# Joining the low-rank query and key weights behind the seventh unit of the first token block instead of the second

## The chip, the cores and the metric

The kernel runs on one core of a Trainium2 chip. The metric is the device time of one execution in microseconds (us), as the median of several runs. The engines are TensorE (PE), whose weight loads are listed apart (PEld), VectorE (DVE), ScalarE (ACT), GpSimd (POOL) and SyncE (SP), which issues nearly all transfers here.

## What is computed

Two layers over 256 context tokens and 2048 latent tokens of width 1024. Each layer normalises and modulates its input (`adaLN`: a shift and a scale from a small matrix product with `w_mod`), projects it by one wide matrix `w_in`, feeds three groups of heads (two gated linear recurrences and one latent attention), and projects the gated results back, with a gate on the sum. The part that matters here is the latent attention's query and key:

```python
def mla_qkv(zcq, zckv, zkr, q_norm_g, kv_norm_g, w_uq, w_ukv, rope):
    q = (rms_norm(zcq, q_norm_g) @ w_uq).reshape(B, L, MLA_HEADS, MLA_QK)
    kv = (rms_norm(zckv, kv_norm_g) @ w_ukv).reshape(B, L, MLA_HEADS, MLA_NOPE + MLA_DV)
    q_nope, q_rope = q[..., :MLA_NOPE], q[..., MLA_NOPE:]
    k_nope, v = kv[..., :MLA_NOPE], kv[..., MLA_NOPE:]
...
    s = jnp.einsum('bqhd,bkhd->bhqk', q, k).astype(F32) * MLA_SCALE
```

The kernel never forms `k_nope`. It multiplies the two low-rank weights of a head once per layer, (256 x 128) times (128 x 128), and scores the 256-wide query latents against the 128-wide key latents through that product. This product is what the change moves.

## The kernel before

Each layer has three stages: `project` (L270), `mix` (the recurrences and the attention) and `output`. Matmul operands are kept as a high and a low half (`hh`/`hl` of the tokens, `wh`/`wl` of the weights), and a product is three matmuls: high x high, high x low, low x high. `split` (L75) makes the halves: a cast on ScalarE (L79), a subtract on VectorE (L85).

`project` takes the tokens in pairs of 128-token tiles, nine pairs in three blocks of three. The columns of `w_in` are cut into twelve groups of up to 256. A unit is one group for the three pairs of a block; the first block's first unit takes groups 0 and 1 together, so its unit `i` is group `i + 1`. A group and a pair make 48 matmuls into one psum tile `pj` of four (L421, or L432 for groups 2 to 5, whose result is transposed). ScalarE or VectorE empties it (L452, L457, L458, L465, L478) and SP stores it. The weights of the next group are loaded as two `wraw` tiles (L355) and split one unit ahead. Behind groups 4, 6 and 8 of a block the next block's pairs are prepared (`normed_pair`): load `xt` (L366), normalise on VectorE (L369 to L375), transpose on TensorE (L383) into one of two psum tiles with the tag `tr`, from which ScalarE writes the modulated `hf` (L390); then `split_pair` makes `hh` (L81) and `hl`. Group 0 also starts the decay gates of one recurrence (`gla_decay`, L587 to L591): for each direction VectorE, ScalarE twice, VectorE (L590), ScalarE (L591).

In layer 0 two more things go on beside the first block. `mod_rest` (L164) computes the rest of the modulation on VectorE: 64 pieces `wmt` of 128 x 512 (L184, three buffers) are loaded one after the other, and each is reduced by L187 (twice for the first 48, once for the rest). After the first sixteen pieces VectorE adds a bias (L192) and SP writes the layer's gate by two transfers (L194), each of 1024 single elements of 4 bytes to scattered addresses:

```python
                for i in range(2):
                    nc.sync.dma_start(out=S0["gate"][i].rearrange("(k p) -> p k", p=P), in_=mc[:, 0:8, i])
```

And `latent_weights` (L240) loads `uq` (L244, in one of the three `xt` buffers), `uk` (L246) and `ur` (L248, both in `stg` buffers of the pairs' results), multiplies (`pw`, L254; the trace shows sixteen records for the eight matmuls) into two psum tiles, also of the tag `tr`, and splits the product into `mh`/`ml` and `ur` into `urh`/`url`. Its results are used first in `mix` (L854, L866).

A scheduler sets the order on each engine from its own estimate of time, with the program's order as priority; SP's queue is worked in order, and at most eight of its transfers are under way.

Of the kernel before, what the change touches and what calls it, by code (L numbers as in the profile page):

```python
# [54 lines left out]
class Trunk:  # L55
# [214 lines left out]
    def project(self, l, S, after):  # L270

        nc, io = self.nc, self.io
        with ExitStack() as ctx:
            R = Route(lambda: self.pool(ctx), "hh hl", "stg gcat gq gkv",
                      "zaT ltn lkd zn zh ltt lqn jk ss rsk rsq ropt ropa ropb gxs gab",
                      "srow wmt jkm mp mc bmc bmd gcol pad", "wraw", "xt st mv ve rs hf", "wh wl")
            ps = Route(lambda: self.pool(ctx, psum=True), "tz", "pj", "tr", "px")
            npair = self.ntiles // 2
            blocks = [list(range(p0, min(p0 + 3, npair))) for p0 in range(0, npair, 3)]

            units = [(b, gs) for b in range(len(blocks))
                     for gs in ([(0, 1)] if b == 0 else [(0,), (1,)]) + [(g,) for g in range(2, self.NGROUP)]]
            h, hf, w, side = {}, {}, {}, iter(())
            if l == 0:
                nc.gpsimd.memset(R.tile([P, 32], F32, name="pad")[:, 0:1], 0.0)
                bm = self.mod_first(S, R, ps, lambda: hf.update({0: self.normed_pair(l, S, R, ps, 0, plain=True)}))
                side = self.mod_rest(S, after, R, bm)
                for g in range(2):
                    w[0, g] = self.group_weights(l, R, g, first=True)
                self.modulate(S, hf[0], 0)  # L290
            else:
                pad = R.tile([P, 64 * 64 + 40], F32, name="pad")
                nc.gpsimd.memset(pad[:, 0:1], 0.0)
                with self.tc.high_priority(offset=self.EARLY):
                    w[0, 0] = self.group_weights(l, R, 0)
                    hf[0] = self.normed_pair(l, S, R, ps, 0)
                    w[0, 1] = self.group_weights(l, R, 1)
                    h[0] = self.split_pair(R, hf[0], hi_eng="act")
                    if len(blocks[0]) > 1:
                        hf[1] = self.normed_pair(l, S, R, ps, 1)  # L300
                        h[1] = self.split_pair(R, hf[1], hi_eng="act")
            self.gate_weights(l, S, R)
            if l > 0:
                self.lower_bounds(S)
            for nm, n in (("gcat", 512), ("gq", 256), ("gkv", 128)):
                S[nm] = R.tile([P, n], F32, name=nm)
                nc.sync.dma_start(out=S[nm], in_=io[nm][l:l + 1, :].to_broadcast([P, n]))
            for pr in blocks[0]:
                if pr not in hf:
                    hf[pr] = self.normed_pair(l, S, R, ps, pr)  # L310
                if pr not in h:
                    h[pr] = self.split_pair(R, hf[pr])
            for i, (b, gs) in enumerate(units):
                nxt = blocks[b + 1] if b + 1 < len(blocks) else []
                j, r = divmod(gs[0] - (self.NGROUP - 8), 2)
                norm = r == 0 and 0 <= j < len(nxt)
                if norm:
                    hf[nxt[j]] = self.normed_pair(l, S, R, ps, nxt[j])
                    if j == 0:
                        h[nxt[0]] = self.split_pair(R, hf[nxt[0]])  # L320
                if i + 1 < len(units):
                    bn, gn = units[i + 1]
                    w[bn, gn[0]] = self.group_weights(l, R, gn[0])
                use = [self.group(l, S, R, ps, g, w.pop((b, g)), h, blocks[b]) for g in gs]
                for j, pr in enumerate(blocks[b]):
                    for u in use:
                        next(u, None)
                    if gs[-1] == self.NGROUP - 1 and j + 1 < len(nxt):
                        h[nxt[j + 1]] = self.split_pair(R, hf[nxt[j + 1]])
                for u in use:  # L330
                    for _ in u:
                        pass
                if i == 1:
                    self.latent_weights(l, S, R, ps)
                if b > 0 and not norm:
                    next(side, None)
                    next(side, None)
            for _ in side:
                pass
# [886 lines left out]
```

## Time and profile before

| | us |
|---|---|
| median of 3 runs (lowest, highest) | 3754.92 (3752.4, 3761.37) |
| the profiled execution's own time | 3755.9 |
| its span | 3754.2 |
| TensorE busy | 3612.3 |
| VectorE busy | 2139.7 |
| ScalarE busy | 1435.5 |

The mean granted clock of TensorE is 0.986 of full speed. Times in the trace count from the start of the span; in a timeline a row's bracket tells how long the engine had stood idle before it, and what ended that. Layer 0's projection goes to about 440 us, layer 1's starts near 1970.

### The profile page before, as it was taken

The page shows a single profiled execution, that of the slowest core. Times are in us where ns is not written, and L with a number is a line of the kernel's source. Part 1 is how long each engine was busy: PE and PEld are TensorE (multiplying, and loading weights), DVE is VectorE, ACT ScalarE, POOL GpSimd, SP SyncE. Part 2 cuts the span into 40 slices and gives each one's busy share as a digit, 9 for nine tenths or more (in the row PEclk, how much of TensorE's full clock was granted, in tenths as well). Part 3 has the DMA queues.
Part 4 walks back from the last instruction along what each step waited for, and adds up shares of the span by engine and source line. Part 5 has one row for each costly group of instructions (what it writes and reads, how often), then busy time and mean ns, then how long its engine had stood idle before and what let it go on. Part 6 is the DMA issues. An engine that isn't in the chain of part 4 may idle for free. (4 is left out here: it accounts for less than half of the span.)

```text
span 3754.2 us, 84546 instructions
## 1 busy us (share of the span) xinstructions
PE 3612.3 (96%) x36056; PEld 3264.7 (87%) x36056; DVE 2139.7 (57%) x5026; ACT 1435.5 (38%) x2296; POOL 811.6 (22%) x617
## 2 busy tenths in 40 slices
PE   8999999999999999998999999999999999999999
PEld 5899999888888888887879999998888888888787
DVE  6764242566666666656765442525665566656566
ACT  3525242344444444443115342523443444444400
POOL 1000000001335354341110000000022344644211
PEclk9999999999999999998999999999999999999999
DMA  7774344322122111116435443433221121221342
GB/s 253 234 202 145 126 132 143 111 81 91 49 69 84 56 61 62 55 43 206 153 110 170 146 152 108 154 120 113 83 90 43 60 68 57 78 78 44 102 143 101
DMA packets 263689, 410.79 MB, mean 109 GB/s; under 512 B 39633, under 2 KB 179985, under 8 KB 262289
## 3 DMA queue, kind: packets, MB, share of 16 engines
q1 hardware_dynamic: 261872, 403.04, 33.8%
q8 instruction: 283, 4.64, 0.5%
q10 hardware_dynamic: 1440, 2.36, 0.2%
q14 instruction: 94, 0.76, 0.1%
HBM read 288.66 MB, written 116.67 MB: 108 GB/s over the span
## 5 line engine op out<-in xcount | busy, mean ns | idle before, releaser
L421 PE MATMUL pj<-wh,hl 128*128 128x256 f32 (+1 forms) x2224 | 622.2, 280 | 7.9 <-DVE hl L85 7.9
L421 PE MATMUL pj<-wh,hh 128*128 128x256 f32 (+1 forms) x2224 | 623.9, 281 | 1.7 <-DVE ve L373 1.2
L421 PE MATMUL pj<-wl,hh 128*128 128x256 f32 (+1 forms) x2224 | 622.7, 280 | 0.1
L911 DVE TENSOR_SCALAR_CACHE_REDUCE sx<-pss 128x512 f32<-128x512 f32 (+1 forms) x648 | 402.9, 632 | 206.1 <-PE pss L909 181.7
L85 DVE TENSOR_TENSOR pl<-ptp,ph 128x512 fp32r<-128x512 f32 x580 | 389.5, 687 | 187.5 <-ACT ph L79 184.2
L79 ACT CAST ph<-ptp 128x512 fp32r<-128x512 f32 x580 | 327.9, 586 | 363.7 <-PE ptp L947 358.3
L421 PEld LDWEIGHTS pj<-wh,hl 128*128 128x128 f32 x2224 | 420.1, 189 | 8.7 <-DVE hl L85 8.6
L421 PEld LDWEIGHTS pj<-wh,hh 128*128 128x128 f32 x2224 | 421.1, 189 | 1.8 <-DVE ve L373 1.6
L421 PEld LDWEIGHTS pj<-wl,hh 128*128 128x128 f32 x2224 | 421.0, 189 | 0.6 <-issue 0.6
L947 PE MATMUL ptp<-ident,sx 128*128 128x128 f32 x2320 | 372.9, 279 | 25.4 <-DVE pl L85 15.8
L934 PE MATMUL oc<-ph,cnh 128*128 128x256 f32 x1160 | 339.6, 315 | 22.7 <-ACT ph L79 22.0
L921 ACT ACTIVATE sx<-sx,nm 128x2304 f32<-128x2304 f32 (+1 forms) x136 | 288.4, 2121 | 184.2 <-DVE nm L917 183.7
L432 PE MATMUL pj<-hh,wh 128*128 128x256 f32 x1136 | 317.3, 279 | 0.0
L947 PEld LDWEIGHTS ptp<-ident,sx 128*128 128x128 f32 x2320 | 273.2, 142 | 50.4 <-DVE pl L85 20.2
L432 PE MATMUL pj<-hh,wl 128*128 128x256 f32 x1136 | 316.2, 278 | 0.0
L432 PE MATMUL pj<-hl,wh 128*128 128x256 f32 x1136 | 315.8, 278 | 0.0
L934 PE MATMUL oc<-ph,cnl 128*128 128x256 f32 x1160 | 301.9, 283 | 0.0
L85 DVE TENSOR_TENSOR wl<-wraw,wh 128x1024 fp32r<-128x1024 f32 (+1 forms) x144 | 169.4, 1211 | 230.6 <-ACT wh L79 230.5
L905 PE MATMUL pss<-cth,qh 128*128 128x512 f32 (+1 forms) x648 | 264.9, 409 | 13.7 <-DVE sx L911 13.7
L934 PEld LDWEIGHTS oc<-ph,cnh 128*128 128x128 f32 x1160 | 222.1, 191 | 51.7 <-ACT ph L79 37.9
L939 PE MATMUL oc<-pl,cnh 128*128 128x256 f32 x1160 | 242.9, 291 | 0.0
L906 PE MATMUL pss<-ctl,qh 128*128 128x512 f32 (+1 forms) x648 | 242.9, 375 | 0.0
(253 smaller groups left out, 7888.0 us busy)
## 6 DMA issues: line engine op xcount, KB each, us to landing
wraw<-in_w_in_dram SPq DMA_DIRECT2D x132, 512.0 KB, 4.5
dnat<-stg SPq DMA_DIRECT2D x104, 256.0 KB, 2.1
vg<-dnat SPq DMA_DIRECT2D x17, 1024.0 KB, 6.1
yt<-dy SPq DMA_DIRECT2D x34, 512.0 KB, 3.6
wmt<-in_w_modT_dram SPq DMA_DIRECT2D x64, 256.0 KB, 4.0
fa<-dF SPq DMA_DIRECT2D x18, 768.0 KB, 4.5
ka<-dK SPq DMA_DIRECT2D x18, 768.0 KB, 4.2
dK<-stg SPq DMA_DIRECT2D x36, 256.0 KB, 4.6
```

The costliest lines, as they stand in the source:

```text
L79: nc.scalar.copy(hi, src)
L85: nc.vector.tensor_tensor(lo, src, hi, op=ALU.subtract)
L421: nc.tensor.matmul(pj[:, j, :n], h[pr][a][:, k, tk], w[b][:, k, :n], start=(k == 0 and a + b == 0), stop=(k == KD - 1 and a == 1))
L432: nc.tensor.matmul(pj[:, j, :], w[b][:, k, cs], h[pr][a][:, k, :], start=(k == 0 and a + b == 0), stop=(k == KD - 1 and b == 1))
L905: nc.tensor.matmul(pss[:, :n], G["qh"][hp][:, i, tk], K["cth"][:, ks], start=True, stop=False)
L906: nc.tensor.matmul(pss[:, :n], G["qh"][hp][:, i, tk], K["ctl"][:, ks], start=False, stop=False)
L911: nc.vector.tensor_scalar(sx[:, ks], pss[:, :n], SCALE, None, op0=ALU.mult, op1=ALU.max, accum_out=mx[:, nb:nb + 1])
L921: nc.scalar.activation(sx[:, :nk], sx[:, :nk], AF.Exp, bias=nm, accum_out=sm)
L934: nc.tensor.matmul(oc, K[k][:, keys(kc, c)], ph[:, c, :], start=(kc + c == 0 and k == "cnh"), stop=False)
L939: nc.tensor.matmul(oc, K["cnh"][:, keys(kc, c)], pl[:, c, :], start=False, stop=(kc + c == nch - 1))
L947: nc.tensor.transpose(pt[:, c, i, :], pexp[i][:, (kc + c) * P:(kc + c + 1) * P], self.ident)
```

## The change

One number: `latent_weights` is called behind unit 6 (group 7) of the first block in place of unit 1 (group 2), in both layers.

```diff
@@ -330,7 +330,7 @@
                 for u in use:
                     for _ in u:
                         pass
-                if i == 1:
+                if i == 6:
                     self.latent_weights(l, S, R, ps)
                 if b > 0 and not norm:
                     next(side, None)
```

What the scheduler makes of it, in layer 0. On TensorE, `pw` stood before among the matmuls of group 3's first pair, 473 `pj` matmuls into the layer:

```order
L432 MATMUL pj<-hh,wh 128x256
L432 MATMUL pj<-hl,wh 128x256
L254 MATMUL pw<-uk,uq 128x128 x8
L432 MATMUL pj<-hh,wl 128x256
L432 MATMUL pj<-hh,wh 128x256
```

It now stands among those of group 8's first pair, 1193 `pj` matmuls in:

```order
L421 MATMUL pj<-wh,hh 128x256
L421 MATMUL pj<-wl,hh 128x256
L254 MATMUL pw<-uk,uq 128x128 x8
L421 MATMUL pj<-wh,hl 128x256
L421 MATMUL pj<-wh,hh 128x256
```

Between the two, the token transposes of L383 stand where they stood (the second set behind 626 `pj` matmuls, before 623); those of the block's third pair, before ahead of the new place, now stand behind `pw`. In layer 1 `pw` moves alike, to 41 matmuls into group 8.

On SP's queue, around the gate's transfers in layer 0, before:

```order
L184 DMA wmt<-in_w_modT_dram 128x512 x2
L194 DMA gate_86<-mc 128x8x1 x2
L246 DMA uk<-in_ukT_dram 128x4x128
L248 DMA ur<-in_uqr_dram 128x2x256
L184 DMA wmt<-in_w_modT_dram 128x512 x2
L453 DMA dQ_89<-stg 128x512
L355 DMA wraw<-in_w_in_dram 128x4x256
```

and now:

```order
L184 DMA wmt<-in_w_modT_dram 128x512 x3
L194 DMA gate_86<-mc 128x8x1 x2
L184 DMA wmt<-in_w_modT_dram 128x512
L453 DMA dQ_89<-stg 128x512
L355 DMA wraw<-in_w_in_dram 128x4x256 x2
L184 DMA wmt<-in_w_modT_dram 128x512
L467 DMA dK_88<-stg 128x512
L467 DMA dF_87<-stg 128x512
L592 DMA dF_87<-gab 128x3x256
L184 DMA wmt<-in_w_modT_dram 128x512 x3
```

`uk` and `ur` are gone from here; `wraw` and `wmt` pieces move up. The two now stand behind the 58th `wmt` piece, among the stores of group 7's results (`dnat`):

```order
L184 DMA wmt<-in_w_modT_dram 128x512 x4
L485 DMA dnat_90<-stg 128x2x256
L184 DMA wmt<-in_w_modT_dram 128x512 x5
L246 DMA uk<-in_ukT_dram 128x4x128
L248 DMA ur<-in_uqr_dram 128x2x256
L485 DMA dnat_90<-stg 128x2x256
L184 DMA wmt<-in_w_modT_dram 128x512 x2
```

Before, the same stretch reads alike without the two. `uq` moves from behind the fourth `wmt` piece to behind the decay gates' stores, and the token tile that follows it is loaded that much earlier, so that two more tiles are normalised on VectorE ahead of L192.

On ScalarE, from the second direction's decay gate to the first `hf`, now:

```order
L588 ACTIVATE gab<-gab 128x768
L589 ACT_TABLE_LOAD
L589 ACTIVATE gab<-gab 128x768
L591 ACT_TABLE_LOAD
L591 ACTIVATE gab<-gab 128x768
L79 CAST wh<-wraw 128x1024 x2
L457 ACT_TABLE_LOAD
L457 ACTIVATE stg<-pj 128x512
L458 ACTIVATE stg<-pj 128x512
L390 ACTIVATE hf<-pt,shT_85,scT_84 128x256 x4
```

The sequence was the same before, with an L457 and L458 between L589 and L591, and six `hf` at its end.

## Rows read from the trace of the kernel before

**Rows 1.** The page, part 1: busy us, share of the span, instructions.
```profile
PE 3612.3 (96%) x36056; PEld 3264.7 (87%) x36056; DVE 2139.7 (57%) x5026; ACT 1435.5 (38%) x2296; POOL 811.6 (22%) x617
```

**Rows 2.** Waits of TensorE, 0 to 440 us: total us, times, longest us.
```profile
PE pw L254 <- DMA uk<-in_ukT_dram: 9.3, 1, 9.3
PE pt L383 <- DVE xt L375: 2.4, 1, 2.4
PE pj L421 <- DVE hl L85: 1.7, 2, 1.5
```

**Rows 3.** Timeline of TensorE, 112 to 132 us: start us, length us, engine, line.
```profile
126.00 3.75 PE L254 MATMUL pw<-uk,uq 128*128 128x128 f32 x16 [9.29 <-DMA uk<-in_ukT_dram]
129.41 0.56 PE L432 MATMUL pj<-hh,wl 128*128 128x256 f32 x1
```

**Rows 4.** Windows: stretch and its length; PE, PEld, DVE, ACT, POOL; PEclk, DMA, GB/s.
```profile
128.00:130.00 2.00, 2.00 (x12) 2.00 (x11) 1.99 (x6) 0.80 (x2) 0.00 (x0) 0.50 1.08 384
130.00:132.00 2.00, 2.00 (x18) 2.00 (x18) 1.30 (x3) 1.97 (x3) 0.00 (x0) 0.94 1.08 380
200.00:300.00 100.00, 99.46 (x854) 99.27 (x853) 55.19 (x133) 24.27 (x43) 3.56 (x5) 1.00 0.68 178
```

**Rows 5.** Timeline of TensorE in layer 1, 2014 to 2022 us.
```profile
2018.10 1.95 PE L254 MATMUL pw<-uk,uq 128*128 128x128 f32 x16
2019.80 0.37 PE L432 MATMUL pj<-hl,wh 128*128 128x256 f32 x1
```

**Rows 6.** Timeline of SP's queue, 103 to 131 us: the issues.
```profile
111.18 1.52 SPq L194 DMA_DIRECT2D gate<-mc  x2
112.75 0.90 SPq L246 DMA_DIRECT2D uk<-in_ukT_dram  x1
```

**Rows 7.** Transfers, 105 to 130 us: GB/s in 40 slices; KB each, us to landing.
```profile
GB/s 331 313 344 292 293 359 334 300 210 226 180 34 15 12 1 0 0 0 0 25 70 28 20 23 19 22 29 38 40 66 74 157 192 377 410 392 393 383 383 387
...
uk<-in_ukT_dram SPq DMA_DIRECT2D x1, 256.0 KB, 13.1
...
gate<-mc SPq DMA_DIRECT2D x2, 4.0 KB, 12.6
```

**Rows 8.** Tile `uk` in layer 1, 1700 to 2100 us.
```profile
DMA to landing us min/median/max: 3.3/3.3/3.3
```

**Rows 9.** Timeline of VectorE, 106 to 150 us.
```profile
121.36 0.69 DVE L187 SCALAR_TENSOR_TENSOR jkm<-wmt,srow 128x512 f32<-128x512 f32 x1 [3.99 <-DMA wmt<-in_w_modT_dram]
...
135.68 1.28 DVE L369 BATCH_NORM_STATS2 st<-xt 128x6 f32<-128x512 f32 x2
...
138.02 0.96 DVE L590 SCALAR_TENSOR_TENSOR gab<-gxs,gab 128x768 f32<-128x768 f32 x1 [1.06 <-ACT gab L589]
```

**Rows 10.** Timeline of TensorE: token transposes near 148 and near 217 us.
```profile
147.98 0.60 PE L383 MATMUL pt<-ident,xt 128*128 128x128 f32 x4
...
217.38 0.60 PE L383 MATMUL pt<-ident,xt 128*128 128x128 f32 x4
```

**Rows 11.** Timeline of ScalarE, 110 to 152 us.
```profile
141.70 0.85 ACT L591 ACTIVATE gab<-gab 128x768 f32<-128x768 f32 x1
...
146.72 2.92 ACT L390 ACTIVATE hf<-pt,shT,scT 128x256 f32<-128x256 f32 x6
```

**Rows 12.** Timeline of VectorE: the first `hh` of the next block, and L187 of piece 55.
```profile
148.69 0.69 DVE L81 CAST hh<-hf 128x1024 fp32r<-128x1024 f32 x1 [0.35 <-ACT hf L390]
...
220.83 0.68 DVE L187 SCALAR_TENSOR_TENSOR jkm<-wmt,srow 128x512 f32<-128x512 f32 x1
```

**Rows 13.** Timeline of SP's queue, 206 to 224 us.
```profile
215.09 5.51 SPq L184 DMA_DIRECT2D wmt<-in_w_modT_dram  x5
...
221.55 0.33 SPq L184 DMA_DIRECT2D wmt<-in_w_modT_dram  x1
```

**Rows 14.** The page, part 6: the `wmt` pieces, KB each, median us to landing.
```profile
wmt<-in_w_modT_dram SPq DMA_DIRECT2D x64, 256.0 KB, 4.0
```

**Rows 15.** Waits of VectorE, 185 to 222 us: total us, times, longest us.
```profile
DVE jkm L187 <- DMA wmt<-in_w_modT_dram: 5.8, 6, 2.0
```

## The prediction

> **What bounds the kernel now.** I read the page's busy times first. TensorE is busy 96% of the span [rows 1], so time is won only where TensorE stands still, or runs slowly, and lost only where it is made to. I then read what TensorE waited for from 0 to 440 us, the first layer's projection [rows 2]. The joined weights (`pw`, L254) waited 9.3 us for the transfer of `uk`; nothing else that the change could reach is over 2.4 us. The timeline [rows 3] shows the spot: nothing for 9.29 us, from 116.71 on, then sixteen `pw` matmuls from 126.00, and group 3's matmuls again from 129.41. The windows [rows 4] show the tail of it: the granted clock is 0.50 (1.2 GHz) from 128 to 130, 0.94 in the next two us, and TensorE is full later (99.46 of the 100 us from 200 on). In layer 1 the same sixteen matmuls follow their neighbours without a wait and take 1.95 us [rows 5].
>
> Why was `uk` late? SP's timeline [rows 6] has the two `gate` transfers just ahead of it: 2 x 1024 elements of 4 bytes, scattered. In the DMA view [rows 7] the traffic falls to 0 to 34 GB/s behind them, then climbs to some 390; 4 KB take 12.6 us to land, and `uk`, issued at 112.75, takes 13.1. In layer 1 it takes 3.3 [rows 8]. So `uk` is not slow, it is behind the gate scatter. The same scatter holds a `wmt` piece that VectorE needs at once: its L187 waited 3.99 us, to 121.36 [rows 9].
>
> **What the change removes.** At the old place: 9.29 us of waiting. The sixteen matmuls took 129.41 - 126.00 = 3.41 us at half clock, against 2019.80 - 2018.10 = 1.70 at full clock: 1.7 more. The next four `pj` matmuls lost 0.45. Together 11.4 us [rows 3, 5]. The matmuls themselves are only moved (1.70 us in either place), as are their two casts, two subtracts, and `urh`/`url` on ScalarE and VectorE, which run beside TensorE. That is also the most this change could give: 0.30% of the 3755.9 us of the profiled execution.
>
> **What moves with it.** (a) `uq` goes on SP's queue from far ahead of the gate scatter to far behind it. It shares three buffers with the token tiles, so a token tile is loaded and normalised earlier. VectorE then does some 2 us of normalisation (1.28 for a tile's statistics [rows 9], the rest for its scaling) ahead of the gate's addition (L192): the scatter starts some 2 us later, at about 113.3. Other splits move ahead: the 1.5 us that TensorE waited for `hl` [rows 2] shrinks by 0 to 1.5; I take 0.7.
>
> (b) **The wait that comes in its place, at L383.** TensorE, freed from `pw`, reaches the second set of token transposes early. Before, these ran at 147.98 [rows 10], 18.6 us after the restart at 129.41; without the pause they come at 116.7 - 0.7 + 18.6 - 0.45 + 0.35 (three matmuls more stand ahead of them) = 134.5. They need a psum buffer that ScalarE empties by `hf`. ScalarE is not free then. Its order is second-direction L591, two weight casts, L457 and L458, then `hf`; before, this took 146.72 - 141.70 = 5.0 us up to `hf` [rows 11]. L591 waits for VectorE's L590 (138.02 before [rows 9]), which stands behind the L187s in VectorE's own order, and those wait for `wmt` pieces held by the scatter. The scatter now starts 2 us later, so the first held piece lands at about 121.36 + 2 = 123.4. The pieces issued behind it come with two `wraw` of 512 KB and the `dK`, `dF` stores, 2.6 MB at 390 GB/s = 6.7 us after the scatter's end at about 127.5: the piece that L590 stands behind is there at some 134.5. Three L187 (0.7 each) and L590 (0.96) bring 138.0, L591 139, casts and L457/L458 143.2, two `hf` 144.2, with the hand-over 144.5. So TensorE waits about 144.5 - 134.5 = 10.0 us, and loses 2.1 us of clock behind it, as it did behind `pw` (1.7 + 0.45). The bounds: no wait at all if VectorE's pieces are not held; 12 us if all runs as late as before.
>
> (c) **`uk` at its new place.** It stands behind the 58th `wmt` piece, before that behind the 19th. Each piece takes one of three buffers, so the 58th is issued when VectorE has done the 55th: in the trace, L187 at 220.83 [rows 12], issue at 221.55 [rows 13]; `uk` would follow at 221.9. VectorE's chain, however, starts earlier now: the cast of `hh` that follows the first `hf` ended its wait at 148.69 [rows 12] and comes at about 145.8 (144.2 and the rest of four `hf`), 2.9 earlier. The work from there to the 55th piece is 2.7 us less, since the two normalisations lie behind us. The issue: 221.9 - 5.6 = 216.3. Landing after 3.3 [rows 8] to 4.0 (the median of a `wmt` piece of the same 256 KB [rows 14]): 219.6 to 220.3; I take 219.9, as layer 1's `uk` itself is nearest but `wmt` pieces are on the queue here.
>
> TensorE's arrival: `pw` stands 1193 `pj` matmuls into the layer, in the first pair of the ninth group. From the transposes at 147.98 to 217.38 [rows 10], which is two matmuls short of it, are 69.4 us; less 0.8 for a set of eight transposes that moves behind `pw`, plus 0.2: 68.8. So 144.5 + 2.1 + 68.8 = 215.4, and a wait of 4.5 us. Then `pw` at half clock, 1.7 more, and 0.45.
>
> By a rule of the Trainium skill, page "DMA: Bandwidth & Descriptors", section on the anatomy of one DMA, a transfer takes about 2.0 us and its bytes over 436e3 per us: 2.6 us for 256 KB, an estimate for another issuing path. The trace does not agree (3.3 and 4.0); by the page's figure the sum would be 0.7 us smaller.
>
> (d) Layer 1: no `wmt` and no gate scatter; `uk` lands in 3.3 us [rows 8], the use is 41 matmuls (about 5 us) into the group. I cost it at nothing; the cover is about 5 us between landing and use. If it is gone, the price is at most 3.3 + 2.1 us.
>
> (e) In the attention and at the layers' ends some fifty stretches of TensorE's order are permuted, with counts equal. No row prices that: 0, with 4 us to either side, a third of the largest pause above.
>
> **Sum.** -9.3 - 1.7 - 0.45 - 0.7 (old place and start) + 10.0 + 2.1 (L383) + 4.5 + 1.7 + 0.45 (new place) = +6.6, say +7. The profiled execution took 3755.9, 1 us above the median of 3754.92; on the median: 3762.
>
> **Rivals.**
> 1. *The wait is simply gone.* VectorE's chain is not held as I think, so `hf` is in time, and `uk` is landed before 203. For it: a piece of the size of `uk` lands in 4.0 us at the median and the removed wait is real [rows 2, 14]. Against: `uk` then sits behind 39 more pieces on one queue, paced by VectorE, and [rows 13] show them issued until 221. It gives -11.4 - 0.7 + 2 = about -10: 3745, just within 0.3%.
> 2. *Break-even.* The L383 wait stands and `uk` is in time (VectorE's chain gains over 10 us instead of 5.6). 6.6 - 4.5 - 1.7 - 0.45 = 0: 3755.
> 3. *Slower.* VectorE's chain gains nothing. It decides by one point, whether L187 of the 55th piece ends earlier than 220.83 [rows 12]. If it doesn't, `uk` lands at 221.9 + 3.8 = 225.7, 5.8 us later than in my sum: +12.8, 3768, over 0.3%. For it: VectorE waited for `wmt` six times in the last 37 us before that point, so a transfer and not its own work may pace it [rows 15]. The Trainium skill, same page, in its rules for kernel authors, advises issuing a DMA early and waiting for it late. The change moves the issue along with the use, so the rule speaks against it; [rows 13] agree as far as they go, since by them and my arrival `uk` would be issued after TensorE is there.
> 4. *It does nothing in one layer.* In layer 1 there is no wait to remove [rows 5], so all effect is in layer 0; if the two layers' permutations outweigh it, +-4 us.
>
> **How the numbers follow.** Forecast (both new waits, +2 to +11) 0.60; break-even 0.16; rival 1 0.10; rival 3 0.14. A measurement of this kernel can tell about 0.3%, 11.3 us. Faster by more needs rival 1 with the permutations in its favour: 0.04. Slower by more: rival 3, and the top of the forecast: 0.19. The rest, 0.77, is within. The range leaves out rival 1's better half and what is beyond rival 3: 3747 to 3769. The forecast's own range is 3757 to 3766.
>
> **What would show it.** Right: no wait for `uk` near 116; a wait of L383 for `hf` or for a psum buffer, 7 to 12 us from about 134 on; the `uk` issue at 214 to 219 and a wait of `pw` of 3 to 6 us there, with granted clock 0.50 behind both; layer 1 without a `pw` wait; SP's `gate` at 112 to 114. Wrong: no wait at L383 (my chain through VectorE's L187s is wrong), `uk` issued before 203 (rival 1), after 221 (rival 3), or TensorE idle in the attention where it was not.

## The result and the profile after

The changed kernel takes 3780.53 us (median of 3 runs, 3774.2 to 3781.94) against 3754.92: 25.6 us more, a ratio of 1.0072 with a 95% interval of 1.0053 to 1.0091. It is slower, by 0.7%. The prediction said 3762, 3747 to 3769, with 0.19 for slower.

The page's first part shows that the loss is idle time. TensorE is busy 2 us more than in [rows 1], and the span is 25.6 us longer (3779.8 against 3754.2):

```profile
PE 3614.3 (96%) x36056; PEld 3266.6 (86%) x36056; DVE 2138.9 (57%) x5026; ACT 1435.7 (38%) x2296; POOL 808.8 (21%) x617
```

TensorE's waits from 0 to 460 us, to be held against [rows 2] (total, times, longest):

```profile
PE pt L383 <- ACT hf L390: 12.6, 1, 12.6
PE pm L149 <- DMA wmod<-in_w_mod_dram: 10.1, 1, 10.1
PE pw L254 <- DMA uk<-in_ukT_dram: 8.0, 1, 8.0
```

The wait near 116 us is gone, and two stand in its place, where the prediction put them. TensorE's timeline has their places ([rows 3, 10] before):

```profile
148.32 1.12 PE L383 MATMUL pt<-ident,xt 128*128 128x128 f32 x4 [12.65 <-ACT hf L390]
```
```profile
227.75 3.78 PE L254 MATMUL pw<-uk,uq 128*128 128x128 f32 x16 [8.03 <-DMA uk<-in_ukT_dram]
```

Behind both, the granted clock (third figure from the end, before the DMA share and GB/s) is at its lower level, 0.50 or 1.2 GHz, as behind the old wait [rows 4]:

```profile
146.00:148.00 2.00, 0.00 (x0) 0.00 (x0) 2.00 (x4) 1.99 (x5) 0.00 (x0) 0.50 0.83 232
...
152.00:154.00 2.00, 2.00 (x11) 2.00 (x11) 2.00 (x8) 0.41 (x1) 0.00 (x0) 0.50 1.04 403
154.00:156.00 2.00, 2.00 (x18) 2.00 (x18) 2.00 (x4) 0.00 (x0) 0.00 (x0) 0.92 1.01 356
...
230.00:232.00 2.00, 2.00 (x12) 2.00 (x11) 1.95 (x6) 0.88 (x2) 0.00 (x0) 0.50 1.08 376
232.00:234.00 2.00, 2.00 (x15) 2.00 (x15) 1.30 (x3) 1.97 (x3) 0.00 (x0) 0.80 1.08 363
```

By these rows TensorE runs at the lower level for some 6.0 us behind the first wait (148.3 to 154.3) and 5.1 behind the second (227.8 to 232.8); behind the old one it was 4.2 (126.0 to 130.2).

SP's queue: the scatter 2.4 us later than in [rows 6], and `uk` at 223.12, not before the 221.9 at which it would have followed in the old trace [rows 13]:

```profile
113.61 1.00 SPq L194 DMA_DIRECT2D gate<-mc  x2
114.71 0.69 SPq L184 DMA_DIRECT2D wmt<-in_w_modT_dram  x1
116.79 0.33 SPq L453 DMA_DIRECT2D dQ<-stg  x1
117.22 1.00 SPq L355 DMA_DIRECT2D wraw<-in_w_in_dram  x2
...
126.44 0.54 SPq L592 DMA_DIRECT2D dF<-gab  x1
...
223.12 0.43 SPq L246 DMA_DIRECT2D uk<-in_ukT_dram  x1
```

VectorE's timeline has the waits of the prediction's part (b), and one that it doesn't name, at L587 for the store of the first direction's `gab`; [rows 9, 12] are the old ones:

```profile
128.97 0.69 DVE L187 SCALAR_TENSOR_TENSOR jkm<-wmt,srow 128x512 f32<-128x512 f32 x1 [7.07 <-DMA wmt<-in_w_modT_dram]
134.33 0.69 DVE L187 SCALAR_TENSOR_TENSOR jkm<-wmt,srow 128x512 f32<-128x512 f32 x1 [3.73 <-DMA wmt<-in_w_modT_dram]
136.65 0.96 DVE L587 SCALAR_TENSOR_TENSOR gab<-gxs 128x768 f32<-128x768 f32 x1 [0.89 <-DMA dF<-gab]
140.95 0.96 DVE L590 SCALAR_TENSOR_TENSOR gab<-gxs,gab 128x768 f32<-128x768 f32 x1 [0.85 <-ACT gab L589]
...
149.21 0.69 DVE L81 CAST hh<-hf 128x1024 fp32r<-128x1024 f32 x1 [1.18 <-ACT hf L390]
...
222.03 0.68 DVE L187 SCALAR_TENSOR_TENSOR jkm<-wmt,srow 128x512 f32<-128x512 f32 x1
```

The last row is L187 of the 55th piece. The store that L587 waits for is held like the others (transfers of 105 to 140 us):

```profile
dF<-gab SPq DMA_DIRECT2D x1, 384.0 KB, 10.1
```

ScalarE's timeline has what follows ([rows 11] before): L591 at 142.23, `hf` at 147.24, and TensorE released at 148.32.

```profile
142.23 0.84 ACT L591 ACTIVATE gab<-gab 128x768 f32<-128x768 f32 x1
...
147.24 1.94 ACT L390 ACTIVATE hf<-pt,shT,scT 128x256 f32<-128x256 f32 x4
```

To see where along the run time goes, I took the start of each matmul after less the start of the same matmul before (the n-th one that writes a given tile), and the median of that over 100 us. I call it the shift. It is +15.0 us from 500 us on, behind layer 0's projection, 16.6 at 1600, 13.9 at 1900, 11.7 at 2300, 9.7 at 3400, and +25.8 from 3600 to the end. So layer 0's projection lost 15, the middle gave back 5, and the last 16 went within 100 us, at the end of layer 1, where the attention's last steps meet the output stage. There TensorE waits (3490 to 3600 us; before, 3480 to 3580, the line for L1101 is missing and the one for `sx` is 3.8):

```profile
PE pzo L1101 <- DVE z L1104: 8.7, 1, 8.7
PE ptp L947 <- ACT sx L921: 5.6, 1, 5.6
```

and VectorE's `z` (3560 to 3600 us) waits for the store of the attention's last `ym`, which frees the memory that `z` takes (before, it waits 2.2 us for it, and TensorE doesn't wait for `z`):

```profile
DVE z L1104 <- DMA dy<-ym: 7.6, 1, 7.6
```

The same store lands in 7.5 us after (first row, 3575 to 3595 us) and 2.3 before (second, 3555 to 3575):

```profile
dy<-ym SPq DMA_DIRECT2D x1, 256.0 KB, 7.5
```
```profile
dy<-ym SPq DMA_DIRECT2D x1, 256.0 KB, 2.3
```

What the scheduler did there, SP's order from the output's weights on, before:

```order
L1062 DMA woraw<-in_w_out_dram 128x1024 x8
L1074 DMA yt<-dy_107 128x1024 x4
L1094 DMA xto<-xs_21445 128x1024 x2
L973 DMA dy_107<-ym 128x512
```

and after:

```order
L1062 DMA woraw<-in_w_out_dram 128x1024 x6
L1074 DMA yt<-dy_107 128x1024 x5
L1094 DMA xto<-xs_21445 128x1024 x2
L1074 DMA yt<-dy_107 128x1024
L973 DMA dy_107<-ym 128x512
```

The last store now has six `yt` ahead of it where it had four. SP's timeline shows what that does, before and after:

```profile
3557.49 0.80 SPq L1094 DMA_DIRECT2D xto<-xs  x2
3563.48 0.32 SPq L973 DMA_DIRECT2D dy<-ym  x1
```
```profile
3553.46 27.70 SPq L1074 DMA_DIRECT2D yt<-dy  x5
3581.78 0.79 SPq L1094 DMA_DIRECT2D xto<-xs  x2
3583.39 0.32 SPq L1074 DMA_DIRECT2D yt<-dy  x1
3583.76 0.42 SPq L973 DMA_DIRECT2D dy<-ym  x1
```

The fifth `yt` is issued only when TensorE's transposes (L1081) have freed its buffer, and the two `xto` stand behind it. So they are issued 2.0 us ahead of the store in place of 6.0, with a `yt` between. SP's waits, 3525 to 3600 us after:

```profile
SPq L1074 <- PE pty L1081: 22.9, 4, 12.7
```

On TensorE, the 48 matmuls of the first output tile (35 before) and 28 transposes of `yt` (16 before) start before the attention's last matmul, so that nothing is left to do while the store lands. The 48 alone don't cost it: e6, e8 and e10 to e13 have them too, with 16 transposes and the `xto` well ahead of the store, and no such wait.

The profiled execution of before is 3 to 6 us above the medians of 13 to 35 runs of it taken beside the experiments (3750.2 to 3753.1); shifts against that trace come out lower than differences of medians by about as much.

### The profile page after: what moved, and what is told of

It is laid out like the page before. It is cut to its first block, busy times and chain, and to the rows that moved or that the text cites. A ratio compares the mean times of both kernels' runs of the same rounds, so it can differ in the third digit from the quotient of the medians.

```text
span 3779.8 us, 84532 instructions
## 1 busy us (share of the span) xinstructions
PE 3614.3 (96%) x36056; PEld 3266.6 (86%) x36056; DVE 2138.9 (57%) x5026; ACT 1435.7 (38%) x2296; POOL 808.8 (21%) x617
```

## The experiments

Two questions: what the 15 us in layer 0 and what the 16 us at the end come from. Theory A: the gate scatter holds TensorE up once or twice in layer 0, and the scheduler's new order costs the end. The rivals are named in each expectation. A table behind the last run has the shifts of all.

**e1 and e2: one layer alone.** `if i == 6:` becomes `if i == (6 if l == 0 else 1):`, and the same with `l == 1`.

> The move in layer 0 alone. Theory A (layer 0's projection loses 15 us by the two new waits, and the scheduler's order at the end of layer 1, which layer 0's move sets, loses 16 more): TensorE waits 12 to 13 us at L383 and 8 us for uk, the end of layer 1 has the wait of L1101 for z of 8 to 9 us, and the time is 3775 to 3790. Rival B (layer 1's own move makes the loss at the end of layer 1): no wait of L1101 over 2 us there, 3765 to 3770.

> The move in layer 1 alone. Theory A: no L383 wait, the old uk wait of 9.3 us near 116 us, no wait of L1101 for z over 2 us at the end, 3750 to 3760. Rival B: the end loses 12 to 16 us as in the changed kernel, 3765 to 3775.

e1: 3784.43 us, ratio 1.0078 (1.0051 to 1.0105): 12.8 us at L383, 9.5 for `uk`, 7.4 of L1101 at the end. e2: 3748.80 us, 0.9990 (0.9980 to 1.0001), with the old wait and a calm end. The move in layer 0 makes both losses, the second 3.4 ms later and through the order that the scheduler gives the end (e6 and e14, below, part this from a mere late arrival). Layer 1's own move costs nothing.

**e3: the last store from another queue.** In the changed kernel, at L973:

```diff
-        nc.sync.dma_start(out=S["y"][...], in_=ym)
+        eng = nc.scalar if nk > CTX and t == self.ntiles - 1 else nc.sync
+        eng.dma_start(out=S["y"][...], in_=ym)
```

> The changed kernel, with the store of each layer's last attention tile issued from ScalarE's queue instead of SP's. Theory A (at the end of layer 1 that store stands on SP's queue behind five yt loads, the first output tile's z waits for it, and TensorE for z): the 8.7 us wait of L1101 falls below 2, the projection is as in the changed kernel (12.6 and 8.0 us of waits), 3765 to 3773. Rival C (the loss at the end comes from output matmuls put in among the attention's, not from the store): the time stays within 4 us of the changed kernel's 3780.5.

3780.67 us, 1.0074 (1.0052 to 1.0096), the time of rival C; the wait of TensorE for `z` (at L1102 here) is still 8.7 us, and the store takes 7.7 us to land. So the store's place on SP's queue is not what delays it. It shares the memory side with two `xto`, a `yt` and the two norm rows, 512 KB each, that are under way with it.

**e4: the scatter from ScalarE's queue.** In the changed kernel, `nc.sync` becomes `nc.scalar` in L194.

> The changed kernel, with the two gate scatters of layer 0 issued from ScalarE's queue instead of SP's. Theory A (the scatter holds what stands behind it on SP's queue, and through VectorE's L187 the hf that L383 waits for): the wmt pieces behind it land in under 6 us, the L383 wait falls from 12.6 to under 4 us, uk is issued 5 to 10 us earlier in relation to TensorE's arrival; projection 8 to 12 us shorter than in the changed kernel, 3765 to 3773. Rival D (the scatter stalls the memory side whatever queue it is on): the waits stay at 12 and 8 us, the time within 4 us of 3780.5.

3780.79 us, 1.0075 (1.0052 to 1.0097), rival D. The transfers from 105 to 140 us:

```profile
wraw<-in_w_in_dram SPq DMA_DIRECT2D x2, 512.0 KB, 20.7
...
dK<-stg SPq DMA_DIRECT2D x1, 256.0 KB, 18.8
...
gate<-mc ACTq DMA_DIRECT2D x2, 4.0 KB, 22.1
```

On its own queue the scatter takes 22.1 us in place of 12.3, and SP's transfers are held just the same. L383 waits 18.0, more than D said, and `pw` 7.2.

**e5 and e8: no scatter.** In the changed kernel and in the one before, the gate's columns are turned into rows on TensorE and stored as 8 rows of 512 bytes; the scheduler puts these stores off to near 380 us, so shape and place of the store change together.

```diff
-                for i in range(2):
-                    nc.sync.dma_start(out=S0["gate"][i].rearrange("(k p) -> p k", p=P), in_=mc[:, 0:8, i])
+                pg = ps.tile([8, 2, P], F32, tag="tz", name="pg")
+                for i in range(2):
+                    nc.tensor.transpose(pg[:, i, :], mc[:, 0:8, i], self.ident)
+                gr = R.tile([8, 2, P], F32, tag="lqn", name="gr")
+                nc.vector.tensor_copy(gr, pg)
+                for i in range(2):
+                    nc.sync.dma_start(out=S0["gate"][i].rearrange("(k p) -> k p", p=P), in_=gr[:, i, :])
```

> The changed kernel without the gate scatter: TensorE turns the 128 x 8 columns into rows and SP writes 8 rows of 512 bytes. Theory A (the scatter itself, whatever its queue, holds the wmt pieces and through VectorE the hf that L383 waits for; and the loss at the end goes with the order of the output's matmuls among the last attention's, which here is as before): L383 waits under 4 us in place of 12.6, the uk wait lies between 0 and 8, no wait of L1101 over 4 us at the end, 3742 to 3758. Rival D (ScalarE's order alone makes L383 late): L383 still waits 9 us or more, 3758 to 3770.

> The kernel before without the gate scatter (rows in place of columns). Theory A: uk lands within 6 us of its issue at about 112, pw waits under 3 us, L383 under 3 us, and the time is 7 to 12 us below before's. Rival D (another load, not the scatter, holds uk): the wait of pw stays over 6 us, no change.

e5 (changed kernel): 3760.60 us, 1.0029 (1.0019 to 1.0039), above A's range by 3 and in the range of rival D, whose sign, a wait of 9 us or more at L383, is missing. TensorE's waits from 100 to 240 us:

```profile
PE pw L259 <- DMA uk<-in_ukT_dram: 9.8, 1, 9.8
PE pt L388 <- ACT hf L395: 2.3, 1, 2.3
```

The L383 wait falls from 12.6 to 2.3, as A said. TensorE is then 12.2 us ahead of before, and waits the longer for `uk` (9.8): the chain of `wmt` pieces does not gain as much as TensorE. The end, in before's order, loses nothing. e8 (before): `uk` lands in 3.3 us, and there is no `pw` wait; the projection is some 10 us shorter. Yet the time is 3753.44, 1.0009 (0.9999 to 1.0018), and A's 7 to 12 us are not there. The shift tells where they go: 3.7 us between 540 and 640 us, without a wait (last section), of which all but 1.2 is back by 1900, and 4.7 between 2300 us and the end (from -9.1 to -4.4), in layer 1's attention and output stage, whose order is permuted again. The -4.4 that is left is about what the trace of before lies above the median beside e8 (3755.9 against 3751.58).

**e6 and e7: `uk` and `ur` loaded at the start of each layer**, into the memory that `url` and `ml` take later (`latent_loads`, called ahead of the first block; `ml` is written behind both `pw`); the matmuls stay where they were in the changed kernel (e6) and in the one before (e7).

```diff
+        uk = c.tile([P, 4, P], F32, tag="url", name=f"uk{l}")
+        nc.sync.dma_start(out=uk, in_=io["ukT"][l].rearrange("h d r -> d h r"))
+        ur = c.tile([P, 2, 2, 256], F32, tag="ml", name=f"ur{l}")[:, 0]
+        nc.sync.dma_start(out=ur, in_=io["uqr"][l].rearrange("(b p) n -> p b n", p=P))
...
+            lat = self.latent_loads(l)
```

> The changed kernel with uk and ur loaded at the start of each layer into memory that their results take later; the matmuls stay at the new place, and the order at the end of layer 1 is nearly that of before. Theory A: no pw wait in either layer, the L383 wait stays at 11 to 13 us, the projection is 3 to 7 us longer than before, nothing is lost at the end: 3750 to 3760. Rival E (the transfers of uk at the new place also cause the L383 wait or the loss at the end): 3738 to 3745, or 3768 and more.

> The kernel before with uk and ur loaded at the start of each layer; the matmuls stay at the old place. Theory A (whatever frees TensorE at 116 us brings it too early to L383): the 9.3 us wait for uk is gone, a wait of 8 to 13 us at L383 takes its place, and the time is within 5 us of before's. Rival F (the L383 wait belongs to the new order on VectorE and SP alone): no wait over 3 us there, 9 to 12 us faster than before.

e7 is the clearest of all: 3750.22 us, 1.0002 (0.9992 to 1.0011). The wait for `uk` is gone, and from 100 to 240 us there is one other, where the old kernel had none, and the shift at 500 us is +0.4:

```profile
PE pt L392 <- ACT hf L399: 9.4, 1, 9.4
```

So the old wait for `uk` was the place where TensorE met the scatter's pause first, not its cause. The Trainium skill ("DMA: Bandwidth & Descriptors", rules for kernel authors) advises to issue a DMA early and to wait for it late. Issued early, `uk` indeed holds nobody up, and yet nothing is won (1.0002). e6: 3770.83 us, 1.0053 (1.0038 to 1.0068), which misses A's range and lies in rival E's; but E's cause isn't there, since L383 waits though `uk` is loaded long before. There is no wait for `uk`, L383 waits 11.2, and a new one takes `uk`'s place, as the psum tiles of `pw` are emptied late by VectorE (160 to 240 us; that its pieces make it late is argued, not tried):

```profile
PE pt L392 <- DVE ml L85: 6.7, 1, 6.7
```

The end, nearly in before's order, costs 3.5 us in place of 16, though TensorE comes there 14.3 us late.

**e9 and e10: `z` elsewhere.** In the output stage's list of pools, changed kernel and before:

```diff
-"gate", "lng lnb", "z", "xto"
+"gate", "z", "lng lnb", "xto"
```

> The changed kernel with the pools of z and of the two norm rows exchanged in the output stage, so that z no longer takes memory next to or on that of the last attention tile's ym; the order at the end of layer 1 becomes that of before. Theory A (15 us are lost in layer 0's projection, 16 at the end, the two are separate): the projection keeps its 12 to 13 and 8 to 10 us waits, no wait of L1101 over 3 us at the end, 3760 to 3770. Rival G (the loss at the end is a consequence of arriving late, whatever the order): 3776 to 3784.

> The kernel before with the same exchange of pools; here the exchange makes the order at the end of layer 1 half like the changed kernel's (two output weights, a store, six more) but with four yt loads ahead. Theory A (what costs is the output's first tile being run ahead of the attention's last steps, and z waiting for the store behind it): within 5 us of before. Rival G2 (the split of the output weight loads costs it): 8 to 16 us slower.

e9: 3757.66 us, 1.0014 (1.0006 to 1.0023), below A's range. The waits of layer 0 stay (11.3 and 8.9), and the end loses nothing (shift +1.0 at 3400, +0.5 at 3700; order and `z`'s place changed together). TensorE comes there only 1.0 us late, so e9 says little of rival G; e6 (late, with little lost) and e14 (early, with 15.2 lost) speak against it. The unforeseen part is at the end of layer 0, where the shift falls from 5.7 at 1600 to -4.4 at 1900. e10: 3748.49 us, 0.9985 (0.9974 to 0.9996): the end bears the split of the weight loads, against G2, and here too 8.3 us are won at layer 0's output, though the last `ym` store lands there in 6.0 us, nearly as late as before (6.3): what counts there is the memory that `z` takes. The time keeps 4.6 of the 8.3. There the kernel before waits for `z` as the changed one does at the end of layer 1 (1690 to 1790 us, before; with the exchange the line is gone):

```profile
PE pzo L1101 <- DVE z L1104: 6.0, 1, 6.0
```

**e14 and e15: unit 5 and unit 2** in place of 6.

> The joining behind unit 5 in both layers; by the scheduler's order the end of layer 1 has five yt loads ahead as in the changed kernel. Theory A (the order at the end costs 14 to 18 us whatever put it there, by z waiting 7 to 9 us for the last store and by a slow clock behind waits): L383 waits 11 to 13, uk 4 to 10, and the end loses 14 to 18: 3772 to 3786. Rival J (the loss at the end belongs to the place of unit 6): no wait of L1101 over 3 us, 3758 to 3768.

> The joining behind unit 2 in both layers: pw stands four matmuls ahead of the place where L383 waits in the changed kernel, and the end of layer 1 has before's order. Theory A (the pause of some 10 us that the scatter causes is met once, wherever TensorE first needs something held by it): one wait of 8 to 12 us at pw and under 3 us at L383, the projection within 4 us of before, 3748 to 3758. Rival K (two waits add, as in the changed kernel): 3762 and more.

e14: 3769.75 us, 1.0048 (1.0035 to 1.0062), a little below its range: the waits in layer 0 are smaller (9.9 and 4.2), while the shift goes from -3.6 at 3400 to +11.6 at 3700. The end costs 15.2 us again under the same order, with

```profile
PE pzo L1101 <- DVE z L1104: 7.6, 1, 7.6
```

So it belongs to the order, not to unit 6 and not to a late arrival. e15: 3763.01 us, 1.0032 (1.0021 to 1.0042), above A's range and in rival K's. It has one wait from 100 to 240 us, as A said and K did not, but a longer one than expected:

```profile
PE pw L254 <- DMA uk<-in_ukT_dram: 15.8, 1, 15.8
```

`uk` was issued at 143.38, behind stores and pieces that the scatter held. The shift at 500 us is +4.7; its profiled execution was its fastest, so the rest of its 12.5 us is not shown by the trace.

**e11, e12 and e13: what can be won.** The move in layer 1 alone with the rows gate (e11), the early loads besides (e12), and e11 with `z` elsewhere (e13).

> The kernel before with the move in layer 1 alone and the gate written as rows. If the parts add (rows gate -10 us in layer 0's projection, of which 3 to 5 were given back by 3.5 us slower matmuls and the attention; the move in layer 1 -2 to -4): 3738 to 3748, faster than both kernels. If the two undo one another: 3748 to 3755.

> As the one before, with uk and ur loaded at the start of each layer besides. No wait for uk is left in either, so by theory A nothing is won by the early loads: within 4 us of the one before. Rival H (the early loads free SP's queue and buffers near 112 us): 4 to 8 us faster than it.

> The move in layer 1 alone, the gate as rows, and z's pool exchanged. If the three parts add by their traces (-10 us in layer 0's projection, -8 at layer 0's output, -2 to -4 in layer 1): 3733 to 3744, below both kernels. If the gains are given back in the attention: 3744 to 3752.

e11: 3750.24 us, 0.9992 (0.9983 to 1.0002); e12: 3753.86, 1.0000 (0.9992 to 1.0009): neither can be told from before, and the early loads win nothing over e11, against rival H. The shift of e11's trace (-13.3 at the end) is of one of its fastest executions. e13: 3741.08, 0.9971 (0.9960 to 0.9982), 9.5 us below the kernel before in the same runs and well below the changed one: it beats both.

Shifts against the trace of before, us (one execution each):

| | at 500 | 1600 | 1900 | 3400 | 3700 |
|---|---|---|---|---|---|
| the change | 15.0 | 16.6 | 13.9 | 9.7 | 25.8 |
| e1 layer 0 alone | 13.3 | 18.4 | 15.6 | 15.5 | 29.6 |
| e2 layer 1 alone | -1.6 | -2.6 | -3.4 | -7.4 | -7.7 |
| e3 store from ScalarE | 11.0 | 9.1 | 9.0 | 8.8 | 24.0 |
| e4 scatter from ScalarE | 19.1 | 14.3 | 11.3 | 8.3 | 26.2 |
| e5 after, rows gate | 1.9 | 5.5 | 5.1 | 4.6 | 4.5 |
| e6 after, early loads | 16.1 | 16.5 | 16.6 | 14.3 | 17.8 |
| e7 before, early loads | 0.4 | -4.5 | -3.8 | -7.1 | -7.0 |
| e8 before, rows gate | -9.6 | -8.6 | -8.7 | -6.2 | -4.4 |
| e9 after, z elsewhere | 8.7 | 5.7 | -4.4 | 1.0 | 0.5 |
| e10 before, z elsewhere | 0.3 | -5.4 | -13.7 | -12.2 | -10.2 |
| e11 layer 1, rows gate | -10.9 | -11.1 | -11.1 | -15.2 | -13.3 |
| e12 layer 1, early, rows | -6.2 | -7.9 | -8.0 | -8.8 | -6.5 |
| e13 layer 1, rows, z | -11.4 | -9.7 | -18.0 | -14.5 | -12.6 |
| e14 unit 5 | 6.5 | 3.6 | 1.3 | -3.6 | 11.6 |
| e15 unit 2 | 4.7 | -0.6 | -1.1 | 1.5 | 0.6 |

The last two columns separate two sets: where the end has the changed kernel's order (the change, e1, e3, e4, e14) it costs 14 to 18 us; where it has not, -0.9 to 3.5.

## Why the prediction was wrong, step by step

- **The old wait (-9.3, -1.7, -0.45): right.** Nothing is left of it near 116 us.
- **L383 (part b): right in place, and in the scatter behind it; the last link was missing and the size too small.** 12.65 us, 10.0 forecast; TensorE came at 135.7 (134.5), release at 148.3 (144.5). VectorE did wait for held pieces: the first held L187 came at 128.97, not 123.4, which took "2 us later" as the whole delay, and waited 7.07 us in place of 3.99 [rows 9]; the next came at 134.33. But the sum goes from a piece at 134.5 by three L187 to the end of L590 at 138.0, and L590 ended at 141.9: that is all of the 3.8 us by which the release was late. What released it was not a piece but ScalarE's L589, which follows from the second direction's L587, and L587 waited last for the `gab` store that the scatter held, to 136.65. That step stands in neither the text of part (b) nor its sum. The clock behind the wait cost some 3.0 us (half of 6.0), 2.1 forecast.
- **`uk` at its new place (part c): the step that failed in layer 0.** "VectorE's chain, however, starts earlier now", by 2.9 us and 2.7 us of work, so an issue at 216.3. It was 223.12. `hh` came at 149.21, 0.5 later than before, and the work that had gone ahead (three token tiles normalised from 149 us to the 55th piece in place of four; one tile more, not two, ahead of L192) came back as waiting: from there to `uk`'s issue VectorE waited 13.5 us for `wmt` pieces (149 to 223.5 us), against 9.3 in the old trace (149 to 222 us):

```profile
DVE jkm L187 <- DMA wmt<-in_w_modT_dram: 13.5, 9, 3.4
```
```profile
DVE jkm L187 <- DMA wmt<-in_w_modT_dram: 9.3, 9, 2.6
```

The transfers pace that chain, not VectorE's work. This is rival 3, at its stated point: L187 of the 55th piece came at 222.03, not before 220.83 [rows 12]. It had a chance of 0.14. That the wait was no more than 8.0 us is owed to the first miss: `uk` was issued 6.8 us later than forecast and took 4.6 us to land, not 3.6, but TensorE, held at L383, came 4.3 us later too (219.7).
- **The projection's sum.** With the measured terms, -9.3 - 1.7 - 0.45, +12.65 + 3.0, +8.0 + 2.5 (half of the time at the lower clock), and +0.6 for `hl` (0.3 less) and a new `pz` wait (0.9): +15.3, against a shift of 15.0. Forecast: +6.6. In kernels with the same move in layer 0 the shift was 8.7 to 15.0 (e1, e3, e9), so a single trace settles it to some 5 us. (A landing in 2.6 us would lower the prediction's sum by 1.0 us, not by the 0.7 that it names, since the sum takes 3.6; `uk` took 4.6.)
- **Layer 1 (part d): right.** No wait for `pw`; e2 and the fall of the shift by 2 us agree.
- **The permuted stretches (part e): the step that made the forecast wrong.** "No row prices that: 0, with 4 us to either side". One of these stretches cost 16.1 us, the middle ones gave back 5. The row that could have priced it was there and not read: the kernel before waits 6.0 us for `z` at layer 0's output, so the wait existed, and whether layer 1 would have it was a matter of which matmuls are left when the attention ends. The order showed six `yt` ahead of the last store, and I had read its start only. Of the 16, 8.7 are the `z` wait and 2.6 the longer waits for `sx` and `ph` (5.6 and 3.4 against 3.8 and 2.6). What is left, some 5, fits the lower clock behind these waits: by the rows below TensorE ran some 6.5 and 3 us at it, and half of that, an estimated 4.7 us, is lost. That division is worked out from rows, not tried alone.

```profile
3550.00:3556.00 6.00, 2.64 (x11) 2.24 (x12) 1.98 (x4) 5.33 (x6) 2.35 (x1) 0.55 0.45 157
3556.00:3562.00 6.00, 5.06 (x26) 4.69 (x26) 2.63 (x5) 2.24 (x4) 0.00 (x0) 0.60 0.51 143
...
3592.00:3598.00 6.00, 5.95 (x20) 4.80 (x21) 5.48 (x9) 0.00 (x0) 1.52 (x1) 0.75 0.29 93
```
- **The ranges.** Rival 3's price was added to nothing from part (e), though the two are independent. With the 16 of the end and the 5 given back, which only the result shows, it comes to 12.8 + 16 - 5 = 24, close to what came.

What stays open: why the `ym` store takes 7.5 us in the new order and 2.3 in the old. e3 rules out its place on the queue. The traffic fits: from 3583.5 to 3591.5 us the transfers ran at 355 GB/s, 2.8 MB, and the store and the five loads of 512 KB under way with it are 2.9 MB. But I didn't try the order with fewer loads beside it, so this is argued.

## What to carry to other kernels

A wait that ends on a transfer may be only the first place that meets a pause made elsewhere: ask what the engine meets next if it comes there early, and whether that hangs on the same cause (e7: 9.3 us won, 9.4 lost). Take the cause away first, here 2048 single elements of 4 bytes to be stored, then move work, and follow the gain to the end of the run: in e8 it was 10 us in the projection and nothing in the time. Price a scheduler's permutations at the ends of stages by the waits that the old trace has at such ends: one edit in the first 6% of a program reordered its last 100 us and lost as much there as where it was made. Look at which memory a stage's first tile inherits: two pool names exchanged won 8.3 us at layer 0's output, of which the time kept 4.6 (e10); with the rows gate and the move in layer 1 alone besides, it was 9.5 (e13).

## What the runs showed of the hardware that I had not expected

The scatter holds transfers of other queues too. From ScalarE's queue, 4 KB took 22.1 us, and 512 KB loads on SP's queue 20.7 (e4), where they take 4.4 without a scatter (e8). The Trainium skill, "DMA: Bandwidth & Descriptors", specifications, says that transfers under 512 bytes are not at line rate, as the engine reads and rewrites; the 12.3 to 22.1 us agree as far as they go. That the others' loads nearly stand still meanwhile is what e4 shows.

TensorE's `pj` matmuls come at one of two spacings, about 113 or 118 ns, for tens of us at a time, both under a granted clock of 1.00 and with no idle time. From 540 to 630 us the kernel before runs at the first, and e8, with the same matmuls, at the second: 797 and 766 of them in 90 us (TensorE's count, first row before, second e8, where three records are missing):

```profile
540.00:630.00 90.00, 90.00 (x797) 90.00 (x795) 26.05 (x34) 31.32 (x48) 0.00 (x0) 1.00 0.53 169
```
```profile
540.00:630.00 90.00, 90.00 (x766) 90.00 (x765) 24.56 (x33) 24.81 (x39) 0.00 (x0) 1.00 0.52 165
```

From 540 to 640 us the shift of e8 goes from -9.9 to -6.2, and it moves by the same 3.7 us in the four others with the rows gate (e5, e11, e12, e13), and not in the change, e7 or e10. What sets the spacing no run here shows.
